# Latent residual rows held in DRAM during the expert stretch, raw value rows in their place, and 4, 3, 3 buffers for the prompt's weight pieces

## The chip, the cores and the metric

One core of a Trainium2 chip runs the whole program in one launch. The metric is the device time of that launch in microseconds (us), the median over runs. The engines are PE (TensorE, matrix products), ACT (ScalarE), DVE (VectorE), POOL (GpSimd) and SP (SyncE, which here only issues DMAs). Each engine executes its own queue in order; a program-wide scheduler fixed these orders when the kernel was built.

## The reference

Two layers of a diffusion trunk work on two streams that share weights: a prompt of 128 tokens and 512 latent tokens (four tiles of 128 rows), all float32, model width 1024. In each layer a stream passes through a norm, one wide input projection, four mixers and sigmoid merge gates, an output projection, and then an expert layer (PEER) with 16,384 experts:

```python
def block(xb):                                   # 128 rows at a time
    q = (xb @ wq).reshape(PEER_BLOCK, PEER_HEADS, 2, PEER_KEY_DIM)
    s = jnp.einsum('phxd,hxnd->phxn', q, keys).astype(jnp.float32)
    ...                                          # top 16 of 16x16 candidates a head -> idx, g
    ue, ve = u[idx], v[idx]
    a = jax.nn.gelu(jnp.einsum('pd,phkd->phk', xb, ue).astype(jnp.float32))
    return jnp.einsum('phk,phkd->pd', (g * a).astype(xb.dtype), ve)

xs = xs + g1 * latent_mixers(modulate(xs, norm1_g[l], sh1, sc1), p, cache_l)
xs = xs + g2 * peer_ffn(modulate(xs, norm2_g[l], sh2, sc2), peer_wq[l], peer_keys[l], peer_u[l], peer_v[l])
```

The prompt's layer does the same with `xp` and without caches. The last residual of both streams is normed once more and is the main output.

## The kernel before, in words

**The latent layer.** `latent_norm`, `latent_mix` and `w_out` compute the mixers and leave the four residual tiles `x1` in the SBUF pool `X`, tag `x4`, four buffers of 4 KB a partition. Filler work, the merge gates (`gate`, L112 to L116, 24 matmuls for each of 32 blocks a layer, with weight pieces `fraw`, `fhi`, `flo`), is spread between the mixers' steps.

**Two ways through the experts.** The prompt and latent tile 0 (`GATHER`) gather the rows they need: `gathered` issues 128 indirect DMAs on the table u and then 128 on v (L1446, on POOL, three buffers `gr`), and DVE reduces each with one instruction (`gr` L1454, `pacc` L1465). Latent tiles 1 to 3 (`DENSE`) go through all 16,384 experts in 128 blocks of 128: `first` multiplies with a block of u (`dA`, 24 matmuls) and `second` with a block of v (`do`, 18 matmuls). Blocks 0 to 67 have their first half done ahead (`AHEAD`); their activations wait in DRAM (`ga`). In `dense`, blocks 68 to 127 come first with both halves, then 0 to 67 with the second half alone.

**Splitting.** Every float32 operand is split into a high part (ACT, L98) and a low part (DVE or POOL, L104, L106) and each product is three matmuls. For the prompt's weights, `streamer` does this piece by piece (128 x 512): a load on SP into `wraw`, then `whi` on ACT, then `wlo` on DVE, then three matmuls. A load can only be issued when its `wraw` buffer is free, so the numbers of buffers bound how far the pieces run ahead.

**Who runs beside whom.** The layer-1 pass of the prompt (`prompt_phase`: mixers `pproj`, branches `pbr`, output `pwo`, queries `pwq`, scores `ps_s`, then `route`, the top-k that ends in the indices `idx`) is written ahead of the layer-0 `dense` and shares the engines with it. Its 160 weight pieces have buffers `(2, 2, 2)` for `wraw`, `whi`, `wlo`. The prompt's layer-1 gathers need its `idx` and run beside the layer-1 latent mix. Tile 0's gathers run in groups of eight (`GRD`), `advance`d from inside `dense` by a budget a block (`DSTEP`). Raw v blocks are loaded into `vr` (two buffers in the pool of `dense`, L1561 to L1563), every second one of the last 68 into the ring `ur` of `experts_in`.

**The end of a dense stretch.** The three accumulators `do` are multiplied with the gate row `g2` and added to `x[t]` (L1595, L1596), tile 0's sum is added on POOL (L1651), and in layer 0 all four are stored to `xl`, in layer 1 normed to the output (`final`, L1716, L1717).

Of the kernel before, what the change touches and what calls it, by code (L numbers as in the profile page):

```python
# [6 lines left out]
F32 = mybir.dt.float32  # L7
F32R = mybir.dt.float32r
# [10 lines left out]
L = 2  # L19
LT = 4  # L20
TL = 512
D = 1024
# [41 lines left out]
TG = 32  # L64
WRB = (2, 3)
OHT = 4
WSCALE = 32768.0
# [6 lines left out]
def trunk(tc, a):  # L74
# [64 lines left out]
    with es:  # L139
# [39 lines left out]
        xp = [dr.tile([128, D], F32, name=f"xp{i}") for i in range(2 * L)]  # L179
        xl = dr.tile([LT, 128, D], F32, name="xl")  # L180
        modd = [dr.tile([2, 2, D], F32, name=f"modd{l}") for l in range(L)]
        gd = [dr.tile([4, KB, 128, TL], F32, name=f"gd{l}") for l in range(L)]
# [631 lines left out]
        def latent_mix(l, m, P, Q, zs, mixf):  # L814
# [457 lines left out]
            def w_out(M, ah):  # L1272
# [29 lines left out]
                for t in range(LT):  # L1302
                    p = psa([128, 512], name="wo")
                    for kb in range(KB):
                        mm3([p], [z[:, kb, t * 128:(t + 1) * 128] for z in ah], [w[kb]], kb == 0, kb == KB - 1)
                    add(t, 1, p)
                    if t == 0:
                        ACT.activation(small([128, 1], "sqrt", 1), ones[:, 0:1], AF.Sqrt)
# [230 lines left out]
        def dense(l, P, first, gen, step, x):  # L1539


            out = [psm([128, 2, 512], name=f"do{i}") for i in range(len(DENSE))]
            LAG = 2
# [14 lines left out]
            def second(n):  # L1558
                g = pend.pop(n)
                own = n >= AHEAD or n % 2 == 0  # L1560
                r, vh, vl = [P.tile([128, 1024], t, name="v" + c, tag="v" + c, bufs=2) if own else first.ring(c)  # L1561
                             for c, t in (("r", F32), ("h", F32R), ("l", F32R))]
                SP.dma_start(r, a[f"v{l}"][n * 128:(n + 1) * 128, :])  # L1563
# [14 lines left out]
            for i, n in enumerate(order):  # L1578
                begin(n)
                if i >= LAG:  # L1580
                    list(second(order[i - LAG]))
                    budget += DSTEP[l][n >= AHEAD] / GRD
                while step < 256 // GRD and (step < budget or i == NB - 1):
                    advance(gen, 1, last(DVE))
                    step += 1
            tail = [second(n) for n in order[NB - LAG:]]
            for q in tail:
                next(q)
            g2 = P.tile([128, D], F32, name="g2", tag="vr", bufs=2)
            SP.dma_start(g2, modd[l][1:2, 1, :].partition_broadcast(128))  # L1590
            for i, t in enumerate(DENSE):
                for q in tail:
                    next(q)
                acc = P.tile([128, D], F32, name="dacc", tag="vr" if i == 0 else "vl", bufs=2)
                DVE.tensor_tensor(acc, flat(out[i]), g2, op=ALU.mult)  # L1595
                DVE.tensor_tensor(x[t], x[t], acc, op=ALU.add)  # L1596
                if l + 1 < L:
                    SP.dma_start(xl[t], x[t])
# [50 lines left out]
        def put_latents(l, x, t):  # L1649
            def put(acc):  # L1650
                POOL.tensor_tensor(x[t], x[t], acc, op=ALU.add)  # L1651
                if l + 1 < L:
                    SP.dma_start(xl[t], x[t])
            return put
# [3 lines left out]
        for l in range(L):  # L1658
# [23 lines left out]
            with pool_right(f"peer{l}") as P, banks(f"pspe{l}", 3, 1):  # L1682
# [3 lines left out]
                with pool_right(f"route{l}") as R:  # L1686
# [4 lines left out]
                    with pool_right(f"wb{l}") as S:  # L1691
                        rt = latent_route(l, S, s)
                    gen, step = gathers(l, (h2n, *rt), modd[l][1:2, 1, :], put_latents(l, x1, GATHER[0]), GRD), 0
                    first = experts_in(l, E, hT)
# [9 lines left out]
                with ein, pool_right(f"dense{l}") as E:  # L1704
                    if l + 1 < L:
                        pr = prompt_phase(l + 1, (2, 2, 2), 1, lambda: None, "left")
                        dense(l, E, first, gen, step, x1)
# [150 lines left out]
```

## Time and profile before

| | |
|---|---|
| median of 3 runs | 4865.96 us (4863.3 to 4877.05) |
| profiled execution, its own time | 4865.31 us |
| its span in the trace | 4863.5 us |
| busy: PE, DVE, ACT, POOL | 4300.6, 3693.9, 2099.0, 2251.7 us |
| moved by DMA | 1231.98 MB, mean 253 GB/s |
| dense stretch of layer 0, about 1690 to 2598 us | PE busy 882.67 us |
| layer-1 mix with the prompt's gathers, about 2790 to 3590 us | PE busy 652.14 us |
| dense stretch of layer 1 | ends with the span |

A busy PE is not a PE at its peak: ends of matmuls are modelled, so spacing from start to start is the better measure of one. Idle time of an engine is listed with what ended it. A stretch is given in us from the start of the span.

### The profile page before, as it was taken

Reading aid. Unit: us, or ns where it says so; the run is one execution under the profiler, and the core shown is the slowest. Engines: PE = TensorE matmul, PEld = TensorE weight load, DVE = VectorE, ACT = ScalarE, POOL = GpSimd, SP = SyncE. Lnnn points to the kernel's source line nnn. Section 1 sums busy time; section 2 is a strip of 40 time slices with the busy share of each in tenths; the row PEclk is TensorE's granted clock in tenths of the full one; section 3 lists DMA queues with packets and bytes.
Section 4 is the critical chain, followed back from the end, with each engine's and each line's share of the span. In section 5 each row is a group of like instructions: output and inputs, shape, how many; then the busy total and the mean of one; then the engine's idle time right before and its main releaser. Section 6 shows DMA issues by size and latency. Waiting matters only on the chain.

```text
span 4863.5 us, 64722 instructions
## 1 busy us (share of the span) xinstructions
PE 4300.6 (88%) x21446; PEld 3545.3 (73%) x21446; DVE 3693.9 (76%) x7389; ACT 2099.0 (43%) x4018; POOL 2251.7 (46%) x1876
## 2 busy tenths in 40 slices
PE   7898988878888899999998878798888888999999
PEld 4565666556778788887887566566677877888887
DVE  4557798777997687777885578877779866777787
ACT  4454424333377544444444253254335763333333
POOL 1023567855654543333332246777566544444232
PEclk9998988889999999999999879888999989999999
DMA  9875876777446899889995277767664579988997
GB/s 320 270 255 189 270 225 214 222 238 245 135 155 247 307 332 317 280 291 315 353 342 187 82 233 257 222 211 234 205 204 128 195 259 326 327 315 314 318 343 253
DMA packets 521126, 1231.98 MB, mean 253 GB/s; under 512 B 53045, under 2 KB 220085, under 8 KB 517717
## 3 DMA queue, kind: packets, MB, share of 16 engines
q1 hardware_dynamic: 373332, 690.90, 42.0%
q0 software_dynamic: 147456, 536.94, 32.4%
q8 instruction: 169, 2.77, 0.2%
q14 instruction: 169, 1.38, 0.1%
HBM read 1136.74 MB, written 90.91 MB: 252 GB/s over the span
## 4 chain that ended last, share of the span: by engine, by line
PE 25%; DVE 22%; DMA 19%; issue 16%; POOL 9%; ACT 1%; SPq 0%; POOLq 0%; DVEq 0%; ACTq 0%
DMA gr<-in_v_dram,idx 10%; POOL gr L1446 6%; DMA gr<-in_u_dram,idx 5%; PE do L112 4%; PE do L114 4%; PE do L116 4%; DVE pacc L1465 3%; DVE gr L1454 2%; DVE oh L1506 2%; PE dA L112 1%; PE dA L114 1%; PE dA L116 1%; DVE wlo L104 1%; DVE oh L1508 1%; POOL flo L106 1%
## 5 line engine op out<-in xcount | busy, mean ns | idle before, releaser
L1446 POOL DMA_INDIRECT gr<-in_v_dram,idx x512 | 648.8, 1267 | 886.5 <-DVE pacc L1465 732.9
L1446 POOL DMA_INDIRECT gr<-in_u_dram,idx x512 | 613.3, 1198 | 708.6 <-DVE gr L1454 542.7
L1465 DVE SCALAR_TENSOR_TENSOR pacc<-gr,wgt,pacc 128x1024 f32<-128x1024 f32 x508 | 720.9, 1419 | 235.6 <-DMA gr<-in_v_dram,idx 232.0
L1454 DVE SCALAR_TENSOR_TENSOR gr<-gr,h2n 128x1024 f32<-128x1024 f32 x512 | 685.8, 1345 | 233.1 <-DMA gr<-in_u_dram,idx 228.3
L112 PE MATMUL dA<-hThi,ul 128*128 128x384 f32 x2048 | 730.0, 357 | 81.4 <-POOL ul L106 77.4
L114 PE MATMUL dA<-hTlo,uh 128*128 128x384 f32 x2048 | 718.1, 351 | 4.0 <-DVE hTlo L104 4.0
L116 PE MATMUL dA<-hThi,uh 128*128 128x384 f32 x2048 | 714.2, 349 | 0.0
L112 PEld LDWEIGHTS dA<-hThi,ul 128*128 128x128 f32 x2048 | 403.5, 197 | 101.4 <-POOL ul L106 90.2
L98 ACT ACTIVATE whi<-wraw 128x512 fp32r<-128x512 f32 (+2 forms) x456 | 274.6, 612 | 456.6 <-DMA wraw<-in_wP_dram 126.3
L104 DVE TENSOR_TENSOR wlo<-wraw,whi 128x512 fp32r<-128x512 f32 (+2 forms) x456 | 336.1, 751 | 145.9 <-ACT whi L98 145.1
L106 POOL TENSOR_TENSOR ul<-ur,uh 128x1024 fp32r<-128x1024 f32 x136 | 333.2, 2452 | 192.6 <-ACT uh L98 191.8
L114 PEld LDWEIGHTS dA<-hTlo,uh 128*128 128x128 f32 x2048 | 403.2, 197 | 11.1 <-DVE hTlo L104 4.7
L116 PEld LDWEIGHTS dA<-hThi,uh 128*128 128x128 f32 x2048 | 401.9, 196 | 1.6
L112 PE MATMUL do<-vh,dwr 128*128 128x512 f32 x1128 | 356.2, 394 | 17.2 <-DVE dwr L104 17.1
L98 ACT ACTIVATE dwr<-dg 128x384 fp32r<-128x384 f32 x256 | 133.9, 523 | 515.9 <-issue 238.6
L116 PE MATMUL do<-vh,dwr 128*128 128x512 f32 x1128 | 355.5, 392 | 0.0
L114 PE MATMUL do<-vl,dwr 128*128 128x512 f32 x1128 | 352.5, 392 | 0.0
L98 ACT ACTIVATE uh<-ur 128x1024 fp32r<-128x1024 f32 x324 | 340.1, 1050 | 21.3 <-DMA ur<-in_uT_dram 20.2
L106 POOL TENSOR_TENSOR flo<-fraw,fhi 128x512 fp32r<-128x512 f32 (+1 forms) x192 | 240.8, 1255 | 194.2 <-ACT fhi L98 148.5
L1533 ACT ACTIVATE dg<-dA 128x384 f32<-128x384 f32 x256 | 124.3, 486 | 440.6 <-PE dA L116 429.5
L1511 ACT ACTIVATE ohl<-oh,w 128x128 f16<-128x128 f16 x768 | 246.7, 399 | 101.6 <-DVE oh L1506 46.3
L112 PE MATMUL gate<-hThi,flo 128*128 128x512 f32 x512 | 229.0, 447 | 39.3 <-DVE th L847 17.3
(570 smaller groups left out, 9817.2 us busy)
## 6 DMA issues: line engine op xcount, KB each, us to landing
ur<-in_uT_dram SPq DMA_DIRECT2D x256, 512.0 KB
vr<-in_v_dram SPq DMA_DIRECT2D x188, 512.0 KB
wraw<-in_wP_dram SPq DMA_DIRECT2D x240, 256.0 KB
wd<-wst SPq DMA_DIRECT2D x24, 2048.0 KB
wv<-wd SPq DMA_DIRECT2D x64, 768.0 KB
w<-in_wmod_dram SPq DMA_DIRECT2D x72, 512.0 KB
ur<-in_v_dram SPq DMA_DIRECT2D x68, 512.0 KB
fraw<-in_wT_dram SPq DMA_DIRECT2D x128, 256.0 KB
```

Source lines behind the costliest of these rows:

```text
L98: ACT.activation(hi, src, AF.Copy)
L104: DVE.tensor_tensor(lo, src, f32(hi), op=ALU.subtract)
L106: POOL.tensor_tensor(lo, src, f32(hi), op=ALU.subtract)
L112: PE.matmul(o, lhsT=ll, rhs=r[0], start=first, stop=False)
L114: PE.matmul(o, lhsT=lh, rhs=r[1], start=False, stop=False)
L116: PE.matmul(o, lhsT=lh, rhs=r[0], start=False, stop=last)
L1446: POOL.indirect_dma_start(out=r, out_offset=None, in_=a[table], in_offset=bass.IndirectOffsetOnAxis(ap=idx[:, c:c + 1], axis=0))
L1454: DVE.scalar_tensor_tensor(r, r, 1.0, h2n, op0=ALU.mult, op1=ALU.mult, accum_out=w[:, c:c + 1])
L1465: DVE.scalar_tensor_tensor(acc, r, w[:, c:c + 1], acc, op0=ALU.mult, op1=ALU.add)
L1506: DVE.tensor_tensor(o[:, 0:2], iota16.unsqueeze(1).to_broadcast([128, 2, 128, OHT]), ob(iT), op=ALU.is_equal)
L1511: ACT.activation(lo[:, j], o[:, 1, :, j], AF.Copy, scale=w32[:, t4 + j:t4 + j + 1])
L1533: ACT.activation(flat(g), p, AF.Gelu_apprx_tanh)
```

## The change

`w_out` stores each finished residual tile to a new DRAM tensor `xs`, and the four `x4` buffers are handed to the raw v blocks `vr` for the dense stretch. The pool of `dense` no longer holds `vr`, which frees 8 KB a partition; the layer-1 prompt's `wraw`, `whi`, `wlo` get 4, 3, 3 buffers for 2, 2, 2, which takes 8 KB. At the end of the stretch the residual tiles are loaded back from `xs`. Since tile 0's load needs one of the `x4` buffers, the last group of eight gathers of tile 0, with the gate row and the add that follow it, is held back until the last block (`i == NB - 1`). The gate row `g2` now lies in a `wv` buffer and the first accumulator product in a `ur` buffer.

```diff
+PB1 = (4, 3, 3)
...
+        xs = [dr.tile([LT, 128, D], F32, name=f"xs{l}") for l in range(L)]
...
                     add(t, 1, p)
+                    SP.dma_start(xs[l][t], x1[t])
...
-                r, vh, vl = [P.tile([128, 1024], t, name="v" + c, tag="v" + c, bufs=2) if own else first.ring(c)
-                             for c, t in (("r", F32), ("h", F32R), ("l", F32R))]
+                if own:
+                    r = X.tile([128, 1024], F32, name="vr", tag="x4", bufs=LT)
+                    vh, vl = [P.tile([128, 1024], F32R, name="v" + c, tag="v" + c, bufs=2) for c in "hl"]
+                else:
+                    r, vh, vl = [first.ring(c) for c in "rhl"]
...
-                while step < 256 // GRD and (step < budget or i == NB - 1):
+                while step < 256 // GRD - (i < NB - 1) and (step < budget or i == NB - 1):
...
-            g2 = P.tile([128, D], F32, name="g2", tag="vr", bufs=2)
+            g2 = P.tile([128, 3 * 512], F32, name="g2", tag="wv", bufs=2)[:, 0:D]
             SP.dma_start(g2, modd[l][1:2, 1, :].partition_broadcast(128))
+            for t in DENSE:
+                x[t] = X.tile([128, D], F32, name="x", tag="x4", bufs=LT)
+                SP.dma_start(x[t], xs[l][t])
...
-                acc = P.tile([128, D], F32, name="dacc", tag="vr" if i == 0 else "vl", bufs=2)
+                acc = first.ring("r") if i == 0 else P.tile([128, D], F32, name="dacc", tag="vl", bufs=2)
...
             def put(acc):
+                x[t] = X.tile([128, D], F32, name="x", tag="x4", bufs=LT)
+                SP.dma_start(x[t], xs[l][t])
                 POOL.tensor_tensor(x[t], x[t], acc, op=ALU.add)
...
+                    x1 = [None] * LT
...
-                        pr = prompt_phase(l + 1, (2, 2, 2), 1, lambda: None, "left")
+                        pr = prompt_phase(l + 1, PB1, 1, lambda: None, "left")
```

The numbers of compute instructions stay the same but for two table loads fewer on ACT; 16 DMAs of 512 KB are added, eight stores and eight loads. The scheduler's order moves a good deal. Line numbers of the changed kernel are a few higher (L113 for L112, L1468 for L1465, L1605 for L1595).

PE, where layer 0's dense stretch ends, before: `do` are the three accumulators, `pbr` and `pwo` the prompt's branch and output products, `paT` its transposes, `nTp` the norm with which the layer-1 latent part begins.

```order
L112 MATMUL do_17568<-uh,dwr 128x512 x2
L114 MATMUL do_17568<-ul,dwr 128x512 x2
L116 MATMUL do_17568<-uh,dwr 128x512 x2
L112 MATMUL do_17569<-uh,dwr 128x512 x2
L114 MATMUL do_17569<-ul,dwr 128x512 x2
L116 MATMUL do_17569<-uh,dwr 128x512 x2
L519 MATMUL paT<-c_ident,pacc__16102 128x128 x8
L112 MATMUL pwo<-whi,plo 128x512
L114 MATMUL pwo<-wlo,phi 128x512
L116 MATMUL pwo<-whi,phi 128x512
```

The same place in the changed kernel, with the prompt's last score product `ps_s` some 100 rows above it:

```order
L117 MATMUL do_17574<-uh,dwr 128x512
L1356 MATMUL ps_s<-kd,pqT 128x128 x4
L117 MATMUL do_17574<-uh,dwr 128x512
...
L113 MATMUL do_17575<-uh,dwr 128x512 x2
L115 MATMUL do_17575<-ul,dwr 128x512 x2
L117 MATMUL do_17575<-uh,dwr 128x512 x2
L284 MATMUL nTp<-diag,x 128x128 x16
L113 MATMUL gate<-hThi,flo 128x512
```

Before, 128 of the prompt's 160 pieces stand ahead of the last `do`, and its output, queries and scores behind it; now all of it stands ahead, and the norm follows the last `do` directly. Between the last `do` and the first latent projection (`projT`) stood 264 gate matmuls, and now 22.

DVE at layer 1's end, before: `dwr` is the split of the gated activations for the last blocks, `dacc` the three gate products, `y` the final norm. No `pacc` stands there.

```order
L104 TENSOR_TENSOR dwr<-dg,dwr 128x384
L104 TENSOR_TENSOR ul<-ur,uh 128x1024
L104 TENSOR_TENSOR dwr<-dg,dwr 128x384
L1595 TENSOR_TENSOR dacc<-do_36109,g_42514 128x1024
L1596 TENSOR_TENSOR x_29337<-x_29337,dacc 128x1024
```

And now:

```order
L105 TENSOR_TENSOR vl<-vr,vh 128x1024
L1468 SCALAR_TENSOR_TENSOR pacc<-gr,wgt,pacc 128x1024
L105 TENSOR_TENSOR dwr<-dg,dwr 128x384
L1468 SCALAR_TENSOR_TENSOR pacc<-gr,wgt,pacc 128x1024
L105 TENSOR_TENSOR ul<-ur,uh 128x1024
L1468 SCALAR_TENSOR_TENSOR pacc<-gr,wgt,pacc 128x1024
L105 TENSOR_TENSOR dwr<-dg,dwr 128x384
L1468 SCALAR_TENSOR_TENSOR pacc<-gr,wgt,pacc 128x1024 x4
L1605 TENSOR_TENSOR ur<-do_36127,g_42534 128x1024
L1606 TENSOR_TENSOR x<-x,ur 128x1024
```

The last eight gathered rows of tile 0 stand among the last two blocks, four of them between the last `dwr` and the first gate product (here named `ur`, after its buffer).

## Rows read from the trace of the kernel before

**Rows 1.** Stretches: length, then busy us of PE, PEld, DVE, ACT, POOL, clock, DMA

```profile
424.00:1212.00 788.00, 668.70 (x3289) 506.43 (x3289) 619.41 (x1055) 309.38 (x687) 496.15 (x451) 0.88 0.74 238
1690.00:2598.00 908.00, 882.67 (x4219) 758.31 (x4218) 719.80 (x995) 383.15 (x580) 318.24 (x230) 1.00 0.89 312
2598.00:2790.00 192.00, 160.55 (x667) 119.77 (x666) 98.55 (x325) 73.72 (x132) 52.85 (x55) 0.85 0.39 128
2790.00:3590.00 800.00, 652.14 (x3249) 508.82 (x3248) 612.32 (x1057) 313.59 (x695) 494.43 (x454) 0.87 0.71 228
```

**Rows 2.** Waits of ACT for `wraw`, 1690 to 2598 us: us in total, times

```profile
  DMA wraw<-in_wP_dram: 96.3, 40
  DMA wraw<-in_wb_dram: 14.5, 4
```

**Rows 3.** Waits of ACT for raw v in the same stretch, us and times

```profile
  DMA vr<-in_v_dram: 2.8, 3
```

**Rows 4.** PE waits, 1690 to 2598 us: us in total, times, longest; first, last

```profile
PE do L112 <- DVE dwr L104: 6.1, 5, 2.3
...
PE dA L112 <- ACT dg L1533: 0.5, 1, 0.5
```

**Rows 5.** PE in order of time: start, us, line, operation, [idle before <- what]

```profile
2597.38 0.64 PE L114 MATMUL do<-ul,dwr 128*128 128x512 f32 x2
2597.85 0.62 PE L116 MATMUL do<-uh,dwr 128*128 128x512 f32 x2
...
2610.07 1.65 PE L282 MATMUL nTp<-diag,x 128*128 128x128 f32 x6 [1.45 <-DVE diag L269]
...
2750.68 2.07 PE L1353 MATMUL ps_s<-kd,pqT 64*128 64x128 f32 x8 [0.69 <-ACT s L591]
2753.44 0.80 PE L112 MATMUL projT<-hThi,wlo 128*128 128x512 f32 x1 [0.69 <-ACT s L591]
```

**Rows 6.** POOL in order of time, about the prompt's layer-1 gathers

```profile
2785.19 1.40 POOL L1422 TENSOR_TENSOR eq<-e,cidx 128x560 f32<-128x560 f16 x1 [1.30 <-DVE idf L1424]
2787.88 1.39 POOL L1422 TENSOR_TENSOR eq<-e,cidx 128x560 f32<-128x560 f16 x1 [1.30 <-DVE idf L1424]
...
2798.14 0.97 POOL L1446 DMA_INDIRECT gr<-in_u_dram,idx  x1 [1.36 <-DVE idx L1426]
...
3590.10 2.35 POOL L1468 TENSOR_TENSOR pacc<-pacc,g 128x1024 f32<-128x1024 f32 x1 [6.71 <-DVE pacc L1465]
```

**Rows 7.** PE's gate matmuls alone: stretch, busy us (count), clock, DMA

```profile
2598.00:2790.00 192.00, 67.83 (x264) 0.85 0.39 128
```

**Rows 8.** DVE's waits for gathered rows, 2790 to 3590 us

```profile
DVE pacc L1465 <- DMA gr<-in_v_dram,idx: 77.8, 54, 4.5
DVE gr L1454 <- DMA gr<-in_u_dram,idx: 54.5, 45, 3.5
```

**Rows 9.** Groups by line: DVE's `pacc`, 2790 to 3590 us, then 4300 to 4800

```profile
L1465 DVE SCALAR_TENSOR_TENSOR pacc<-gr,wgt,pacc 128x1024 f32<-128x1024 f32 x127 | 199.1, 1568 | 79.0 <-DMA gr<-in_v_dram,idx 77.8 <-DVE sm L920 0.4
...
L1465 DVE SCALAR_TENSOR_TENSOR pacc<-gr,wgt,pacc 128x1024 f32<-128x1024 f32 x122 | 156.5, 1282 | 42.1 <-DMA gr<-in_v_dram,idx 41.6
```

**Rows 10.** POOL's `flo` alone, 2598 to 2790 us: busy us (count)

```profile
2598.00:2790.00 192.00, 31.55 (x24) 0.85 0.39 128
```

**Rows 11.** Stretches in the middle of the dense stretch, columns as in rows 1

```profile
2000.00:2300.00 300.00, 284.48 (x1401) 248.99 (x1400) 233.04 (x294) 127.15 (x191) 107.67 (x79) 0.99 0.87 296
2300.00:2500.00 200.00, 199.95 (x868) 162.37 (x867) 165.43 (x207) 82.03 (x121) 68.86 (x43) 1.00 0.98 350
```

**Rows 12.** DVE at the end of layer 1, in order of time

```profile
4840.92 0.56 DVE L104 TENSOR_TENSOR dwr<-dg,dwr 128x384 fp32r<-128x384 f32 x1 [1.86 <-ACT dwr L98]
4847.55 1.22 DVE L1595 TENSOR_TENSOR dacc<-do,g 128x1024 f32<-128x1024 f32 x1 [6.07 <-PE do L116]
```

**Rows 13.** POOL there: tile 0's last group of gathers and its sum

```profile
4793.27 1.68 POOL L1446 DMA_INDIRECT gr<-in_v_dram,idx  x1 [9.75 <-DVE pacc L1465]
...
4821.47 2.59 POOL L1651 TENSOR_TENSOR x<-x,pacc 128x1024 f32<-128x1024 f32 x1
```

## The prediction

> **What bounds the kernel now.** I read the busy times by stretch first, then the engines' waits inside each stretch, then single rows in order of time at the three seams.
>
> The layer-0 dense stretch is PE's: 882.67 of 908 us busy at a granted clock of 1.00 (2.4 GHz) [rows 1]. Nine kinds of PE wait, from 6.1 us down to 0.5, add to 24.6 us there [rows 4]; that is all that better feeding can give back in it. The prompt beside it is bound by its pieces: ACT stood 96.3 + 14.5 = 110.8 us, 44 times, until a `wraw` load landed [rows 2], 2.5 us a time. With two buffers a load goes out only when the piece before the last is split, so its flight is exposed, and the prompt gets through 128 of its 160 pieces before PE's last `do`, which starts at 2597.85 [rows 5].
>
> Then comes a stretch of 192 us in which no engine is full: DVE is busy 98.55 us of it, POOL 52.85, the DMA share is 0.39 [rows 1]. Here the prompt's remaining chain runs (32 pieces, norm, queries, scores, top-k), and the latent part fills in with gates. The prompt's first layer-1 gather goes out at 2798.14 [rows 6], 200 us after the last `do`.
>
> From there to 3590.10, where the last row is in, lie 792 us for 256 rows, 3.1 us each [rows 6]. In that stretch DVE is busy 612.32 us and waits 77.8 + 54.5 = 132.3 us for gathered rows [rows 1, 8]: 745 of 800, 93%. DVE, in order, with the gathers in its queue, is the bound. PE is busy 652.14, at a clock of 0.87. Layer 0's like stretch takes 788 us, with PE busy 668.70, or 85% [rows 1].
>
> So the prompt's end sets when the gathers start, and the gathers with DVE set how long the mix lasts. The two streams meet at no other place.
>
> **The change part by part.** All against the profiled execution: span 4863.5 us, its own time 4865.31, so 1.8 us lie around the span; the median is 0.7 us above that.
>
> *Raw v in four buffers.* ACT waited for `vr` 2.8 us, three times, in the whole layer-0 stretch [rows 3]. Worth at most that; I take 0.
>
> *Prompt pieces with 4, 3, 3.* The exposed flight goes, and the order has every one of the 160 pieces and the scores ahead of the last `do`. Three terms follow.
>
> (a) The dense stretch grows by the work it takes in. 32 pieces are 96 matmuls; two `do` of the same width are 0.47 us apart [rows 5], so 96 x 0.235 = 22.5 us. Eight `ps_s` take 2.07 us [rows 5], 32 take 8.3; the 32 transposes and norm products at the same 0.26 us are 8.3. Sum 39 us. DVE takes in less than the 98.55 us it spent in the seam and goes from 719.80 of 908 (79%) to at most 818 of 947 (86%) [rows 1]; a DVE in order near that loses something to waits. Against it stand parts of the 24.6 us of PE waits. I take +45; bounds +15 (39 less all the waits) and +138 (39 and all of DVE's 98.55 in the open).
>
> (b) The seam shrinks. Before, 200 us from the last `do` to the first gather. Now this lies between: tile 0's last gathered rows, held back to the last block, with the end of the top-k. In layer 1's tail the last `dwr` starts at 4840.92 and the first gate product is held until the first accumulator is done at 4847.55 [rows 12]; the third accumulator follows about 5 us later, so `dwr` leads the last `do` by about 12 us. Behind `dwr` DVE has five rows of `pacc`, each with a step of the top-k; the steps are 2.7 us apart before [rows 6], a `pacc` is 1.28 to 1.57 us [rows 9]: 5 x 4.2 = 21 us, so the rows are in some 9 us after the last `do`. A gate product and add on POOL take 2.35 and 2.59 us by their like [rows 6, 13], steps of the top-k of 1.4 stand between, and three of each come in turn: +16. Tile 0's square, root and diagonal: +5. The norm's transposes, which started 12 us after the last `do` [rows 5] with prompt work in between, take some 22 us with their splits: +43; then the first row, some 55 us after the last `do`. PE has nothing else in the first 21 us of it, since no prompt is left. Term: 55 - 200 = -145; bounds -160 (the old start of 12 plus 28) and -110 (90 us).
>
> (c) The mix gets fuller. Of the seam's 160.55 us of PE [rows 1] 39 were the prompt's; some 15 the norm; the rest, about 107, are gates and projections (gates alone 67.83 [rows 7]; 264 matmuls then, 22 now) that now run beside the gathers. DVE's own share of that is small: by the order 22 more instructions of it stand between first and last gather, some 15 us. If DVE goes on as the bound, +15. If PE can be no fuller there than the 85% of layer 0's like stretch, (652 + 107) / 0.85 = 893, +93 on 800. I take +45, nearer to DVE, since the trace has DVE at 93% and PE idle for 148 us there [rows 1].
>
> A rule bears on this term. A `pacc` beside much POOL work takes 1568 ns, in layer 1's dense stretch, where POOL only gathers, 1282 [rows 9]. The Trainium skill (SBUF — State Buffer, "SBUF: two separate sides") says that VectorE and GpSimd share one pair of ports, locked for a whole instruction, and that a DVE instruction with two SBUF inputs and a GpSimd one that reads SBUF exclude each other; the rows agree with that. The seam's 24 `flo` on POOL, 31.55 us [rows 10], which ran beside an idle DVE, would by it stand in DVE's way: 15 + 29 = 44 us for (c) where 15 would do without it.
>
> *Stores and loads of residual rows.* 16 x 0.52 MB; at 350 GB/s [rows 11] 1.5 us each. The stores run where DMA has room; four v loads that can now go out early, ahead of some query weights, hold these up by 6 us a layer at most. The reloads wait on no slow buffer. Together +3; 0 to +15.
>
> *The held-back group.* Layer 0's is in (b). In layer 1 the group took 28 us from its first gather to its add [rows 13], and all eight rows now stand in DVE's queue ahead of the gate products, which before started at 4847.55. With three rows fetched early the eighth is done some 24 us after the third `dwr` from the end, which is 8 us before the last one: 4857 in old time. The three products and adds then end some 7 us later than before, and behind them three norms. +6; 0 to +12.
>
> Sum: 45 - 145 + 45 + 3 + 6 = -46. 4865.3 - 46 = 4819 us.
>
> The Trainium skill (Perfetto Trace Analysis, "Optimization Strategy") says that the same gap repeating on the engine that should be full can mean too few buffers. Taken for PE alone, that would make this change worth the 24.6 us of rows 4 at most, 4841; the repeating gap of rows 2 is on ACT, for a stream off PE's path, and what it delays is the next stage.
>
> **The rivals.** A difference under 0.3%, 15 us, is no difference here.
>
> *The mix is DVE's and the dense stretch takes the prompt in its gaps.* (a) 35, (b) -145, (c) 15, tails 3: -92, 4773 us. For it: DVE at 93%. Against it: PE would be at (652 + 107) / 815 = 93% there, fuller than in any stretch of this kind.
>
> *PE fills up in the mix.* (c) is 93 and the sum +2: 4867, no change. For it: PE's share stays at 82 and 85% in both mixes. Against it: its clock is granted at 0.87 there and 1.00 in the dense stretch, and its idle time there ends on others.
>
> *Prompt pieces hold up PE in the dense stretch: slower.* The order puts 68 of the pieces within 20 blocks, where 27 stood. Before, about 128 x 300 / 908 = 42 pieces a 300 us went with 296 GB/s [rows 11]; 41 more pieces of 0.26 MB in some 215 us are 50 GB/s more, 346, and the highest row is 350 at a share of 0.98 [rows 11]. A landing then comes later than the place that the order has for its matmul, and PE, in order, stands. If every second of these 68 waits the 2.5 us of rows 2, that is 85 us: 4904. It decides from 46 us on, that is from 0.7 us a piece. For it: the numbers just given, and two software gathers in the same engines. Against it: four loads can be in flight where two were.
>
> *The change does not do what it says*, that is the prompt ends late in spite of the buffers: the order excludes it for the issue; it would show as the slower case.
>
> **How the numbers follow.** Forecast 0.45, with its own range 4785 to 4850; DVE's mix 0.17; PE fills up 0.20; pieces hold up PE 0.18. The range that leaves out 2 in 10 reaches into both sides, 4760 to 4895. Faster by over 0.3%: 0.45 x 0.95 + 0.17 + 0.20 x 0.1 = 0.62. Slower: 0.18 x 0.85 + 0.20 x 0.15 + a little = 0.19. Same: 0.19.
>
> **What would show it.** Right: no `pwo`, `pwq` or `ps_s` after the last layer-0 `do`; that `do` some 45 us later than 2598; the first layer-1 gather of the prompt 45 to 70 us behind it; its last row 820 to 850 us after the first; ACT's waits for `wraw` in the dense stretch well under 110.8 us. A gap of about 20 us on PE behind the last `do`. Layer 1's dense stretch of the old length and a tail some 6 us longer. Wrong: PE waits of `pproj` and `pbr` above 50 us in the dense stretch, or a mix longer than 880 us.

## The result, and the profile after

The changed kernel takes 4785.35 us in the median of 4 runs (4773.14 to 4790.78); its ratio to the kernel before, on the same chip, is 0.9826 (95% interval 0.9812 to 0.984). In a second group of runs it was 0.9819 (0.9796 to 0.9842). It is faster, by 1.7 to 1.8%, as forecast; the size was forecast at 46 us and is about 80. The time lies in the range, 25 us above its lower end, and at the very edge of the forecast's own 4785 to 4850.

The span cut at the same landmarks, from the trace: the first and the last `do` of each layer, the prompt's first gather of layer 1 and its last `pacc` on DVE. "Again" is a second profile of the changed kernel.

| stretch, us | before | after | again | forecast of the difference |
|---|---|---|---|---|
| start to first `do` of layer 0 | 1683.7 | 1674.2 | 1662.4 | 0 |
| dense stretch, layer 0 | 914.3 | 927.9 | 929.7 | +45 |
| last `do` to first gather | 200.1 | 44.6 | 44.0 | -145 |
| layer-1 mix, first gather to last `pacc` | 790.6 | 842.6 | 846.2 | +45 |
| to first `do` of layer 1 | 472.6 | 474.9 | 473.6 | +3 (loads and stores, both layers) |
| dense stretch, layer 1 | 791.1 | 797.2 | 788.6 | 0 |
| behind the last `do` | 11.1 | 21.2 | 18.7 | +6 |
| sum (span) | 4863.5 | 4782.6 | 4763.1 | -46 |

The three stretches of the change, with the columns of [rows 1]:

```profile
1674.20:2602.10 927.90, 918.50 (x4419) 791.80 (x4419) 776.58 (x1270) 419.39 (x646) 325.04 (x255) 1.00 0.90 315
2602.10:2646.80 44.70, 15.93 (x88) 13.39 (x86) 32.58 (x56) 16.95 (x29) 20.27 (x16) 0.69 0.45 152
2646.80:3489.30 842.50, 716.60 (x3609) 561.14 (x3611) 626.74 (x1058) 331.94 (x728) 516.28 (x472) 0.90 0.71 231
```

PE is busy for 918.50 of 927.9 us of the dense stretch: the prompt's work went in and PE's idle time fell to 9.4 us. The second row is what is left of the seam, the third the fuller mix.

ACT's waits for `wraw` in the dense stretch (us, times, longest), 110.8 in [rows 2]:

```profile
ACT whi L99 <- DMA wraw<-in_wP_dram: 30.4, 22, 4.8
```

All waits of PE in that stretch, for [rows 4]:

```profile
PE do L113 <- DVE dwr L105: 4.1, 3, 1.9
PE pproj L115 <- DVE wlo L105: 2.0, 2, 1.7
PE mb L420 <- DVE pC L754: 1.4, 1, 1.4
PE bp L354 <- DVE pouts L105: 0.9, 1, 0.9
PE pbr L113 <- DVE pth L514: 0.7, 1, 0.7
PE pqk L521 <- DVE pn L514: 0.3, 1, 0.3
```

No wait for a prompt piece's landing is among them; the rival in which the pieces hold PE up did not come, although the DMA moves 332 GB/s there, near the 346 which that rival had:

```profile
2300.00:2550.00 250.00, 249.98 (x1112) 203.24 (x1111) 205.77 (x310) 106.83 (x165) 72.75 (x54) 1.00 0.94 332
2550.00:2602.10 52.10, 49.16 (x208) 39.04 (x207) 50.00 (x200) 15.05 (x21) 14.93 (x23) 0.97 0.45 148
```

Over 250 us PE is busy for 249.98. In the last 52 us it is DVE that is full (50.00): the prompt's top-k is there now, with `dwr` and the held rows of tile 0.

The seam on PE, in order of time (start, us, line, operation, idle before it and what ended it), for the first rows of [rows 5]:

```profile
2601.88 0.64 PE L117 MATMUL do<-uh,dwr 128*128 128x512 f32 x2
2629.83 0.55 PE L284 MATMUL nTp<-diag,x 128*128 128x128 f32 x1 [27.32 <-DVE idx L1429]
```

The product reads `diag`, not `idx`; what the wait is for is taken up under (b) below.

And on POOL, for [rows 6]; the top-k's `eq` run to 2627, tile 0's sum is at 2622.53, and the first gather follows the norm:

```profile
2620.07 1.19 POOL L1425 TENSOR_TENSOR eq<-e,cidx 128x560 f32<-128x560 f16 x1
...
2622.53 2.33 POOL L1663 TENSOR_TENSOR x<-x,pacc 128x1024 f32<-128x1024 f32 x1
...
2646.76 1.25 POOL L1449 DMA_INDIRECT gr<-in_u_dram,idx  x1 [0.15 <-issue]
```

DVE's two gather rows in the mix (busy us, mean ns), for [rows 9], and below them its waits for gathered rows, for [rows 8]:

```profile
L1468 DVE SCALAR_TENSOR_TENSOR pacc<-gr,wgt,pacc 128x1024 f32<-128x1024 f32 x126 | 212.9, 1689 | 73.7 <-DMA gr<-in_v_dram,idx 72.7
L1457 DVE SCALAR_TENSOR_TENSOR gr<-gr,h2n 128x1024 f32<-128x1024 f32 x128 | 168.9, 1322 | 68.7 <-DMA gr<-in_u_dram,idx 67.9
```

```profile
DVE pacc L1468 <- DMA gr<-in_v_dram,idx: 72.7, 50, 5.9
DVE gr L1457 <- DMA gr<-in_u_dram,idx: 67.9, 61, 4.4
```

At the end of layer 1, for [rows 12], DVE has the last held row right ahead of the first gate product:

```profile
4758.68 1.29 DVE L1468 SCALAR_TENSOR_TENSOR pacc<-gr,wgt,pacc 128x1024 f32<-128x1024 f32 x1 [1.06 <-DMA gr<-in_v_dram,idx]
4759.88 1.22 DVE L1605 TENSOR_TENSOR ur<-do,g 128x1024 f32<-128x1024 f32 x1
```

That product stood 4.9 us ahead of the last `do` before; now it is 1.5 us ahead.

### The profile page after: what moved, and what is told of

It is laid out like the page before. It is cut to its first block, busy times and chain, and to the rows that moved or that the text cites. A ratio compares the mean times of both kernels' runs of the same rounds, so it can differ in the third digit from the quotient of the medians.

```text
span 4782.6 us, 64650 instructions
## 1 busy us (share of the span) xinstructions
PE 4243.9 (89%) x21446; PEld 3511.5 (73%) x21446; DVE 3699.4 (77%) x7389; ACT 2097.7 (44%) x4016; POOL 2247.6 (47%) x1876
## 4 chain that ended last, share of the span: by engine, by line
PE 27%; DVE 19%; issue 17%; DMA 17%; POOL 11%; ACT 1%; POOLq 0%; SPq 0%; DVEq 0%; ACTq 0%
DMA gr<-in_v_dram,idx 9%; POOL gr L1449 7%; DMA gr<-in_u_dram,idx 4%; PE do L113 4%; PE do L115 4%; PE do L117 4%; DVE pacc L1468 2%; DVE gr L1457 2%; PE dA L113 2%; PE dA L115 1%; PE dA L117 1%; DVE oh L1509 1%; POOL flo L107 1%; DVE e L1423 1%; POOL ul L107 1%
## 5 line engine op out<-in xcount | busy, mean ns | idle before, releaser
L1449 POOL DMA_INDIRECT gr<-in_u_dram,idx x512 | 599.9, 1172 | 719.8 <-DVE gr L1457 598.4
L1468 DVE SCALAR_TENSOR_TENSOR pacc<-gr,wgt,pacc 128x1024 f32<-128x1024 f32 x508 | 743.1, 1463 | 241.2 <-DMA gr<-in_v_dram,idx 238.4
L1457 DVE SCALAR_TENSOR_TENSOR gr<-gr,h2n 128x1024 f32<-128x1024 f32 x512 | 667.3, 1308 | 242.3 <-DMA gr<-in_u_dram,idx 240.6
L113 PE MATMUL dA<-hThi,ul 128*128 128x384 f32 x2048 | 729.6, 357 | 85.2 <-POOL ul L107 84.6
L113 PEld LDWEIGHTS dA<-hThi,ul 128*128 128x128 f32 x2048 | 403.6, 197 | 105.3 <-POOL ul L107 97.2
L113 PE MATMUL do<-vh,dwr 128*128 128x512 f32 x1128 | 358.7, 396 | 19.2 <-DVE dwr L105 19.1
L113 PEld LDWEIGHTS do<-vh,dwr 128*128 128x128 f32 x1128 | 210.4, 189 | 65.0 <-DVE dwr L105 26.2
```

The source lines that it names most:

```text
L113: PE.matmul(o, lhsT=ll, rhs=r[0], start=first, stop=False)
L1449: POOL.indirect_dma_start(out=r, out_offset=None, in_=a[table], in_offset=bass.IndirectOffsetOnAxis(ap=idx[:, c:c + 1], axis=0))
L1457: DVE.scalar_tensor_tensor(r, r, 1.0, h2n, op0=ALU.mult, op1=ALU.mult, accum_out=w[:, c:c + 1])
L1468: DVE.scalar_tensor_tensor(acc, r, w[:, c:c + 1], acc, op0=ALU.mult, op1=ALU.add)
```

## The experiments

Ratios are to the kernel before on the same chip, with 95% intervals. "Stretch" is the layer-0 dense stretch.

**The buffers alone undone.**

```diff
-PB1 = (4, 3, 3)
+PB1 = (2, 2, 2)
```

> The changed kernel with the prompt's layer-1 pieces back in 2, 2, 2 buffers; residual rows leave SBUF and raw v has four buffers as in the change. By the order 128 of 160 pieces stand ahead of the last layer-0 do, and 264 gate matmuls stand behind it, as before the change. Theory (all of the gain is the deeper pieces, the hand-over alone only costs): the seam from the last do to the prompt's first layer-1 gather is 190 to 210 us again, the dense stretch 910 to 920 us with 20 us or more of PE waits, the end of layer 1 some 16 us longer than before: 4870 to 4890 us. Rival (raw v in four buffers is what took the PE waits out of the dense stretch): the stretch is 895 to 903 us and PE waits in it are under 12 us: 4850 to 4868. Second rival (the 9.5 us that the changed kernel was early at its first do come from the hand-over): the first do starts near 1674 us here too; by the first theory it may stand anywhere between 1674 and 1684, as chance of one execution.

Ratio 1.0005 (0.9987 to 1.0023): without deeper pieces nothing is left of the gain. Stretch 908.4, seam 206.0, 21.2 us behind the last `do`; ACT waits 113.8 us for `wraw` again. So the pieces' buffers make the gain, as the first theory had it. But the stretch is 6 us shorter than before and PE's waits are 15.9 us for 25.0, which lies between that theory and the first rival, and the median of 4859.53 us is under the theory's 4870 and in that rival's span. The wait which held rows would shorten, of `do` for `dwr`, fell only from 6.1 to 5.1 us; the rest are single waits of other kinds. Whether raw v in four buffers, the held group or the order did it, this run doesn't show. The first `do`, at 1678.1 us, decides nothing on the second rival.

**Raw pieces in four, split halves in two.**

```diff
-PB1 = (4, 3, 3)
+PB1 = (4, 2, 2)
```

> The changed kernel with 4, 2, 2 buffers for the prompt's pieces: raw pieces in four, split halves in two. By the order the pwo pieces now stand in the dense stretch, the 16 pwq pieces and ps_s behind the last do with 228 gates. Theory (the exposed landing was the only thing that held the prompt: ACT's 110.8 us for wraw): the prompt is as early as with 4, 3, 3 in time if not in order, seam under 90 us, 4785 to 4815 us. Rival (the order decides: what it puts behind the last do stays behind, and two split halves tie the pieces to PE's pace): seam 110 to 150 us, 4825 to 4855 us.

Ratio 0.9868 (0.9852 to 0.9885), most of the gain. No wait of ACT for `wraw` is left at all; what it waits for now are `whi` buffers that PE's products have yet to read (79.8 us on `pproj`, 37 times). Stretch 906.5, seam 132.9 (the rival's 110 to 150), mix 785.7. The rival is right on the seam, the theory on the time, 4792.73 us: what stays in the seam burdens neither the stretch (21 us shorter than with 4, 3, 3) nor the mix (57 us). A seam that is shortened by moving its work pays for that work elsewhere; of the 88 us of seam between the two kernels the time shows some 10 to 20. And the wait for landings, gone here, accounts for 67 of the 155 us by which the change shortens the seam; the other 88 come with the third buffer of the halves.

**No group held back.** Tile 0's sum goes through a gather buffer and DRAM.

```diff
-                while step < 256 // GRD - (i < NB - 1) and (step < budget or i == NB - 1):
+                while step < 256 // GRD and (step < budget or i == NB - 1):
...
-                POOL.tensor_tensor(x[t], x[t], acc, op=ALU.add)
+                POOL.tensor_tensor(r, r, acc, op=ALU.add)
+                SP.dma_start(x0[l], r)
```

> The changed kernel in which tile 0's last group is not held back: its sum is built in a gather buffer, stored to DRAM, and all four residual tiles are read back after the last raw v. Theory (the 27 us of idle PE behind the last layer-0 do and the 21 us behind the last do of layer 1 are the held group on DVE and POOL): seam 45 down to 25 to 30 us, end of layer 1 21 down to 11 to 14 us, the dense stretches as in the changed kernel: 4755 to 4768 us. Rival (the eight rows only move into a stretch where DVE is already 84% busy, and PE waits there instead; the norm behind the finals keeps its place): dense stretch 0 some 8 to 12 us longer, seam 35 to 40: 4772 to 4785 us.

Ratio 0.9806 (0.9782 to 0.983), not told apart from the changed kernel's. Each came true in part: behind the last `do` of layer 1 10.9 us in place of 21.2, as the theory said; the seam 33.9 in place of 44.6, between the two spans; and the stretch 944.4 in place of 927.9, which the theory left as it was and the rival had 8 to 12 us longer. Its last 62 us, in the columns of [rows 1], and its longest kind of PE wait in the whole stretch:

```profile
2550.00:2612.00 62.00, 52.34 (x216) 40.60 (x215) 59.72 (x236) 15.03 (x21) 18.14 (x25) 0.94 0.51 168
```

```profile
PE do L113 <- DVE dwr L105: 14.1, 6, 6.3
```

DVE is full there (59.72 of 62) and PE waits for it, 14.1 us in the stretch where the changed kernel has 4.1. Of the 16.5 us by which the stretch is longer, 8.0 lie in its last 300 `do` (88.1 us for 80.1); the other 8.5 come before, in single waits of an order that differs a little, and I can't put them down to the rows. So the held group takes 8 us or somewhat more out of the stretch and adds 10.7 to the seam. In layer 1, where no top-k of the prompt stands beside, it costs 8 to 10 us and gives nothing that shows.

**Sixteen rows held back**, in the kernel with the hand-over in layer 0 alone (below).

```diff
-                while step < 256 // GRD - (l == 0 and i < NB - 1) and (step < budget or i == NB - 1):
+                while step < 256 // GRD - 2 * (l == 0 and i < NB - 1) and (step < budget or i == NB - 1):
```

> The kernel with the hand-over in layer 0 alone, with two groups, sixteen rows, held back to layer 0's last block. Theory (DVE is full only over the last 50 us of the dense stretch, where the prompt's top-k runs: 50.00 of 52 us; with eight rows held out PE waits are 9 to 11 us, with none held 21.7): another eight held rows leave little to gain, the stretch is 0 to 5 us shorter than 928 to 931, and the seam is 18 to 30 us longer than 44.6: 12 to 28 us slower than with eight. Rival (each row held out of the dense stretch gives it back 2 us, as the first eight did): stretch 912 to 916, and no difference in sum beyond 8 us.

Ratio 0.9877 (0.9849 to 0.9906) against 0.9769 for eight rows: stretch 927.6, seam 65.6, as the theory said. The next eight rows return 2 to 4 us for 21; PE's waits are 8.4 us, hardly under the 9.4 to 11.6 with eight. The credit of the held rows ends where PE's waits do. The whole is 50 us slower, though, not 12 to 28: 19 of it stand between the mix and layer 1's first `do`, in an order taken up below, and 7 in layer 1's dense stretch.

**The prompt's low halves made twice on DVE.**

```diff
+            DVE.tensor_tensor(lo, src, f32(hi), op=ALU.subtract)
             DVE.tensor_tensor(lo, src, f32(hi), op=ALU.subtract)
```

> The changed kernel in which DVE makes each low half of the prompt's layer-1 pieces twice: some 144 to 160 more instructions of 0.6 to 0.7 us, about 100 us more DVE in the layer-0 dense stretch, which puts it at 92 to 94% busy. By the order 16 of the 160 pieces, the queries', now stand behind the last do, as with 4, 2, 2 buffers, so the stretch is to be held against that kernel's 906.5 us, and the seam against its 132.9. Theory 1 (a DVE in order above 85% holds PE up, as I charged for in the forecast): 25 us or more longer, 932 and up, with PE's waits for DVE above 25 us. Theory 2 (DVE runs ahead of PE and has room nearly up to its full time): 903 to 918 us, PE waits under 18 us.

Ratio 0.9879 (0.9835 to 0.9924). The stretch with 4, 2, 2, then this one:

```profile
1684.40:2590.90 906.50, 898.19 (x4321) 776.13 (x4320) 736.41 (x1031) 399.85 (x615) 306.06 (x234) 1.00 0.91 320
```

```profile
1680.10:2590.60 910.50, 899.62 (x4315) 775.26 (x4314) 812.97 (x1173) 400.30 (x611) 388.00 (x234) 1.00 0.91 319
```

DVE goes from 736 to 813 us, 89% of the stretch (I had expected 92 to 94%), and the stretch is 4 us longer with PE waits of 10.6 us for 8.4. Theory 2: at 89% on average DVE holds up next to nothing; it does only where it is full for tens of us, as at the end. The whole time isn't told apart from that of 4, 2, 2.

**One matmul for three in layer 1's gates.**

```diff
+                    if one:
+                        PE.matmul(p, lhsT=hi[:, k4, :], rhs=hT[0][:, kb, :], start=kb == 0, stop=kb == KB - 1)
```

> The changed kernel with one matmul in place of three for each piece of layer 1's gates (the products with the low halves are left out): some 500 matmuls fewer in the layer-1 mix, 143 us of PE busy time by the rows of 144.82 us for 504. All splits and gathers stay. Theory 1 (PE's share is what ends at 82 to 85% in a mix: the gates that the change moved in there lengthened it): from the first to the last gathered row (717 - 143) / 0.85 = 675 us or, if DVE takes over on the way, under 760 in place of 842; about 4700 us. Theory 2 (DVE with its gathers is the bound, as I had it in the forecast): 785 to 830 us, 4730 to 4775 us.

**The gates' low halves from ACT.**

```diff
+        if lo_eng == "act":
+            ACT.activation(lo, src, AF.Copy)
```

> The changed kernel in which the low halves of layer 1's gate and branch pieces are written by a copy on ACT in place of a subtraction on POOL (their values are not the low halves then): some 100 POOL instructions and 137 us of POOL leave the layer-1 mix, as many of about 0.6 us go to ACT, 60 us. Theory 1 (POOL's work beside DVE stretches DVE's own instructions): the row of pacc falls from 1.69 to 1.45 to 1.55 us, that of the first product from 1.32 towards 1.25, and the mix is 25 to 60 us shorter than 842; 4725 to 4760 us. Theory 2 (POOL's subtractions cost DVE nothing that counts, the gathers' landing and PE set the pace): both rows within 5%, mix 830 to 850; 4775 to 4795 us.

Ratios 0.9768 (0.9738 to 0.9797) and 0.9774 (0.9744 to 0.9804). The mix of each, first the one with fewer matmuls, then the one with copies on ACT:

```profile
2648.10:3462.00 813.90, 653.00 (x3131) 506.47 (x3132) 634.79 (x1059) 337.33 (x735) 521.67 (x472) 0.81 0.72 240
```

```profile
2647.80:3470.40 822.60, 713.58 (x3658) 563.54 (x3658) 573.43 (x1058) 381.06 (x830) 386.87 (x379) 0.91 0.71 238
```

With 498 gate matmuls fewer, PE's busy time fell by only 64 us, since the granted clock fell from 0.90 to 0.81, and the mix by 29; that is in Theory 2's span, and PE is 80% busy, so no fixed share of PE ends the mix. With POOL freed of 129 us DVE's own busy time fell by 53 us, and the mix by 20: waits for gathered rows rose from 140.6 to 160.1 us. The rows of DVE are in Theory 1's span, the mix is 5 us short of it. Neither PE nor POOL is the bound by itself. DVE's two gather rows in the kernel with copies on ACT, to be held against 1689 and 1322 ns above:

```profile
L1470 DVE SCALAR_TENSOR_TENSOR pacc<-gr,wgt,pacc 128x1024 f32<-128x1024 f32 x126 | 186.3, 1478 | 79.0 <-DMA gr<-in_v_dram,idx 77.9
L1459 DVE SCALAR_TENSOR_TENSOR gr<-gr,h2n 128x1024 f32<-128x1024 f32 x128 | 157.0, 1227 | 82.5 <-DMA gr<-in_u_dram,idx 82.2
```

**Hand-over in layer 0 alone.** Layer 1 keeps its residual rows in SBUF and holds no group back.

```diff
-                while step < 256 // GRD - (i < NB - 1) and (step < budget or i == NB - 1):
+                while step < 256 // GRD - (l == 0 and i < NB - 1) and (step < budget or i == NB - 1):
...
-            for t in DENSE:
+            for t in (DENSE if l == 0 else ()):
```

> The changed kernel with the hand-over of residual rows and the held group in layer 0 alone; in layer 1, where no prompt runs beside the dense stretch, residual rows stay in SBUF and raw v has its two buffers as before the change. Theory (layer 1 only pays: 6 us in its dense stretch for rows that no longer go out between and 10 behind its last do): from the first to the last do 790 to 793 us, 11 to 12 us behind it: 4768 to 4775 us. Rival (the 6 us of the dense stretch are chance or come with the earlier part of the layer): only the 10 behind the last do come back, 4774 to 4780 us.

Ratio 0.9788 (0.9769 to 0.9807): behind the last `do` 11.1 us, and, not expected, 456.0 us from the last `pacc` to the first `do` of layer 1 where the changed kernel took 474.9; the time, 4752.41 us, is under both spans. It was run again, beside the changed kernel unaltered:

> The kernel with the hand-over in layer 0 alone, a second profile of it. Its layer 1 took 456.0 us from the last gathered row of the prompt to the first do where the others took 470 to 475. Theory (chance of one execution, as in the kernel with half groups, whose layer 1 is the same up to the size of a group and took 471.1): 465 to 475 here, and the time is 8 to 14 us under the changed kernel's on the same chip. Rival (residual rows that stay in SBUF take 17 us out of that stretch): 452 to 460, and 22 to 32 us under it.

> The changed kernel unaltered, a second profile of it, beside the next three. To tell chance from effect: the first do of layer 0 stood at 1667.6 to 1684.4 us in kernels whose program up to there is the change's, the layer-1 dense stretch at 788.7 to 797.2 with the same order. Theory (the 9.5 us by which the changed kernel was early at its first do and the 6 us by which its layer-1 dense stretch was longer are chance): first do anywhere from 1667 to 1685, layer-1 dense stretch 788 to 795; the layer-0 dense stretch 926 to 932, seam 41 to 46, mix 838 to 848, 18 to 21.5 us behind the last do. Rival (they belong to this program): 1672 to 1677 and 795 to 799 again.

The kernel with the hand-over in layer 0 alone: 4751.95 us, 0.9769 (0.9745 to 0.9794), with 455.0 us in that part; the changed kernel beside it: 4774.65. So it beats both kernels, by 23 us the changed one. The rival's numbers came true, so the 455 is no chance, but it doesn't come from rows that stay in SBUF: the kernel with sixteen rows held has the same layer-1 source and took 473.9, the last of the next two 470.1. The order of instructions there differs from kernel to kernel, and PE's waits for `oh` with it (26.1 us, against 36.7 and 33.1). That is about half of the difference; which place of the order decides I did not separate. Some 8 to 10 of the 23 us are the held group of layer 1, most of the rest this order.

The changed kernel's second profile settles another point: its layer-1 dense stretch is 788.6 us, so the 6 us more of the first profile were chance. Its first `do` stood at 1662.4, below the 1667 to 1685 expected, where the first profile had 1674.2.

**Half groups.** Groups of four, in both layers, then in layer 0 alone; the diff is the second's. `AST` starts a group twice as often ahead of the dense stretch.

```diff
-AST = (45, 4)
+AST = (45, 2, 4)
...
-GRD = 8
+GRD = (4, 8)
```

> The kernel with the hand-over in layer 0 alone, and tile 0's gathers in groups of four for eight, so that only four rows are held back to the last block. Theory (the held rows, 3.5 us each with a step of the top-k, are the 27 us of idle PE behind the last layer-0 do): seam 44.7 down to 28 to 36 us, dense stretch of layer 0 up by at most 6, from 4752 to 4738 to 4750 us. Rival (as with no held group at all, what leaves the seam lengthens the dense stretch as much, or smaller groups cost on ACT and DVE): 4750 to 4765 us.

> The kernel with the hand-over in layer 0 alone, and groups of four rows for eight in layer 0 alone, layer 1 as in the run before it. Theory (half the held rows shorten dense stretch and seam of layer 0 together by 12 us, as one profile had it: 922.8 + 37.9 for 931.3 + 44.6): 955 to 966 us for both, and 8 to 15 us under the kernel with groups of eight. Rival (that was chance): 968 to 977 for both, no difference beyond 6 us.

Ratios 0.9811 (0.9778 to 0.9844) and 0.9809 (0.9784 to 0.9834); neither is ahead of the kernel with groups of eight. The first, 4765.44 us, came out at the end of its rival's span. Seam 37.9 and 37.8, where 28 to 36 had been expected of the first; stretch 922.8 and 930.7: together 960.7 and 968.5, against 975.9 and 974.7 in the two profiles of the kernel with groups of eight. The second lies in its rival's span, but not its time, 4773.89 us, 22 more than with groups of eight. Its first `do` stood at 1697.8 us, 24 later, in an order that is its own, and the part ahead of layer 1's first `do` took 470.1 for 455.0, so the gain of 7 us in the stretch and the seam was lost outside them.

## Why the prediction was right, and where its sizes failed

The direction, the cause and the main term held: the prompt was bound by the buffers of its pieces, the order takes all 160 of them into the dense stretch, and the seam shrinks. With 2, 2, 2 buffers none of it is left. The prediction named one cause, the exposed landing; by 4, 2, 2 there are two, since with no landing exposed the queries and scores still stood behind the last `do`, until the halves had a third buffer. Of the total's miss of 35 us, 31 are term (a). Term by term:

**(a) The dense stretch, +45 forecast, +13.6 and +15.4 measured.** This term failed: it was mis-sized by 30 us and crossed its lower bound of +15 in the first profile. In the trace it is some 29 us more of busy PE less 16 us of waits. Three things in it were wrong. First, "DVE in order near that loses something to waits": DVE was at 84% and PE's waits fell from 25.0 to 9.4 us; with DVE driven to 89% the stretch grew by 4 us. Second, the step on the held-back group: I charged its eight rows to the seam and gave the stretch they left no credit. Without the hold the stretch is 944.4 us, 30 over before, so up to 16.5 us were to be credited, 8.0 of them seen over its last 300 `do`. Third, the scores: I took 2.07 us for eight `ps_s` from a row in the seam, where the granted clock was 0.85; in the stretch, at 1.00, eight take 1.16:

```profile
2533.90 1.16 PE L1356 MATMUL ps_s<-kd,pqT 64*128 64x128 f32 x8
```

That is 4.6 us for 32 in place of 8.3; the transposes and norm products had been priced from the same row. The rest of the sum comes out near: 39 less 3.7 for the scores and less 3.3 for PE's waits (25.0 before, with a tenth kind of 0.4 us that the prediction left out, and 21.7 without the hold) is 32, and the stretch without the hold grew by 30.

**(b) The seam, -145 forecast, -155.5 and -156.1 measured.** 44.6 us are left where I had 55, and that the total is this close is luck in part: its two halves miss in opposite directions. The term has the norm begin 21 us behind the last `do` and the first gather go out 34 us after that; measured are 27.7 and 16.9. The held rows took longer: four `pacc` behind the last `dwr` take 2.17 us each, not 1.28 to 1.57, with the gate products between them, so the last row is in 15.6 us behind the last `do`, not 9. And the term's last step, from 43 to 55 us, had no row: in the trace the gather goes out on POOL 0.15 us after the norm's last split there.

What does the norm wait for? The profile puts the 27.32 us down to `idx`, but `nTp` reads `diag`, which stands right beside `idx` in DVE's queue:

```profile
2629.41 0.28 DVE L271 TENSOR_SCALAR diag<-c_ident,rstd 128x128 f32<-128x128 f32 x1
2629.60 0.22 DVE L1429 CAST idx<-idf 128x128 int32<-128x128 f32 x1
```

With sixteen rows held `idx` is done 26 us before the norm begins, and the wait is longer and ends on `diag`:

```profile
2624.50 0.22 DVE L1430 CAST idx<-idf 128x128 int32<-128x128 f32 x1
...
2650.44 5.11 PE L284 MATMUL nTp<-diag,x 128*128 128x128 f32 x24 [48.30 <-DVE diag L271]
```

So it is tile 0's sum, then its square and root, that the norm waits for; the top-k only stands between them in the queues of DVE and POOL. With no held row the norm begins 15.3 us behind the last `do`, 12.4 us sooner, of which 10.7 reach the first gather.

**(c) The mix, +45 forecast, +52.0 and +55.6 measured.** The size held; the reason did so in part. What lengthens the mix is the work that came from the seam: in the four kernels with 504 or 528 gate matmuls in it (before; with 2, 2, 2; with 4, 2, 2; with the low halves made twice) it takes 785.7 to 801.4 us, in all with 747, but for the two experiments on it, 837.2 to 852.1. How it does so stays open in part. I set the value between a DVE bound (+15) and a PE bound (+93), "nearer to DVE". The two experiments bear out neither: 143 us less PE work by the rows at the old clock gave 29 us, 129 us less POOL gave 20. On DVE the 52 us are 21.5 more of busy time, 8 of waits for gathered rows and 31 of waits for ACT (18.8 before, 49.7 after), less 9 of other waits; no run varied those for ACT by themselves.

With POOL's subtractions gone `pacc` takes 1478 in place of 1689 ns and the first product 1227 in place of 1322, 26.6 + 11.9 = 38.5 us of DVE over the 254 rows; for that 93 `flo` left POOL, 118.9 us, and the mix gave back 20. The rule of the Trainium skill (SBUF — State Buffer, "SBUF: two separate sides") that I weighed there agrees with these durations. The 29 us that I put on (c) for 24 `flo` don't: they had no working ([rows 10] has 31.55 us of POOL), and in proportion, as an estimate, 24 of the 93 would be worth 5 of the 20 us. In the change itself the two rows together went only from 378.7 to 381.8 us, since the first product, in this row of before, became shorter:

```profile
L1454 DVE SCALAR_TENSOR_TENSOR gr<-gr,h2n 128x1024 f32<-128x1024 f32 x128 | 179.6, 1405 | 56.5 <-DMA gr<-in_u_dram,idx 54.5 <-issue 1.4
```

The other rule of the Trainium skill that I weighed (Perfetto Trace Analysis, "Optimization Strategy": the same gap again and again on the engine that should be full can mean too few buffers), taken for PE alone, had 4841 us. PE's waits fell by 15.6 us; of the 155 us of the seam 67 came with the gap that repeated on ACT, as 4, 2, 2 shows, the rest with the halves' buffers.

**The tail and the residual rows.** +6 forecast for layer 1's end; 10.1 and 7.6 measured; the kernels without a held group in layer 1 have 10.9 to 12.1 us behind the last `do`, as before the change. Loads and stores: +3 forecast; the part from the mix to layer 1's first `do` is 2.3 and 1.0 us longer.

**What stays open.** The first `do` of layer 0 stood at 1683.7 before and at 1674.2 and 1662.4 after. Of ten further profiles of kernels whose PE order up to there is the change's, eight spread from 1662.4 to 1680.1; two, in which the last rows differ, stand at 1678.1 and 1684.4. The value before lies at the upper edge of that. The change alters the order of layer 0's mix a little, and with one profile of before I can't exclude that some of the 9.5 or 21.3 us is its doing. Buffers of 2, 3, 3, the halves' alone, were not run.

Of the rivals the nearest was the mix that is DVE's (4773): its total is close, but for the wrong reason, since it had +15 for a mix that took +52.

## What to carry to other kernels

When work moves into a stretch that another engine fills, what counts is not the average share of the engine beside it but whether there is a part of tens of us where it is full: here DVE at 84 to 89% cost next to nothing over 850 us, and cost PE 9.6 us over the last 62 where no row was held out of them. An instruction that is held back is charged where it goes and credited where it came from; credit it only as far as the waits that it caused. And before a few us are put down to an edit, look whether the order elsewhere has changed: kernels with the same layer-1 source differed there by 14 to 19 us, and the shortest of them was so in both of its profiles. And an engine's wait is put down to the last thing that came; look whether the instruction reads it.

## What the runs showed of the hardware

The granted clock took back more than half of what fewer matmuls gave: 143 us of matmul work by its rows were left out of the mix, the clock fell from 0.90 to 0.81 (between the levels 1.2 and 2.4 GHz), and PE's busy time fell by 64 us. The gates alone, in the changed kernel and in the one with fewer matmuls:

```profile
2646.80:3489.30 842.50, 209.93 (x747) 0.90 0.71 231
```

```profile
2648.10:3462.00 813.90, 80.07 (x249) 0.81 0.72 240
```

So the gates took 130 us less, and PE's other matmuls, 2862 and 2882 of them, 572.9 us where they had taken 506.7.

The gathers' issue on POOL became dearer when DVE got more subtractions of two SBUF operands. In the layer-0 dense stretch the same 128 issues took 1331 ns each, and 1938 with every low half made twice (first the kernel with 4, 2, 2, then that one; busy us, mean ns); before, after, with 2, 2, 2 and with no group held they took 1320 to 1501:

```profile
L1449 POOL DMA_INDIRECT gr<-in_v_dram,idx x128 | 170.3, 1331 | 372.1 <-DVE pacc L1468 345.3 <-DVE pacc L1466 8.8 <-DMA gr<-in_v_dram,idx 7.7
```

```profile
L1452 POOL DMA_INDIRECT gr<-in_v_dram,idx x128 | 248.1, 1938 | 297.9 <-DVE pacc L1471 261.3 <-DMA gr<-in_v_dram,idx 13.6 <-DVE pacc L1469 7.4
```

It cost nothing that shows here: DVE's waits for gathered rows in that stretch fell from 90.4 to 55.3 us.
